# Where the squares of a head norm are split: at the end of each third, with root and product per half

## The chip, the cores and the metric

The kernel runs on one core of one Trainium2 chip. The metric is the device time of one execution in microseconds (us). Before the change it is 837.59 us, the median of three runs (837.31 to 838.25).

A core has five engines with a queue of instructions each, which they work through in order: TensorE (matrix products; its weight loads are shown apart as PEld), VectorE (DVE), ScalarE (ACT), GpSimd (POOL) and SyncE, which here only issues DMAs. Matrix products write to PSUM; this kernel uses four single PSUM banks (`bk0` to `bk3`) in turn, and two double ones for attention scores (`sc`).

## The reference

Two transformer-like layers work on 512 latent tokens and 256 context tokens of width 1024. The change lies in the first layer's mixer, differential attention with eight heads:

```python
def diff(qq, kk, vv, gate):
    o1 = sweep_attention(qq[..., 0, :], kk[..., 0, :], vv)
    o2 = sweep_attention(qq[..., 1, :], kk[..., 1, :], vv)
    o = o1 - lam.astype(o1.dtype) * o2
    o = rms_norm(o, subln_g) * (1.0 - lam_init)
    o = o.reshape(o.shape[0], o.shape[1], BRANCH_WIDTH)
    return (o * jax.nn.silu(gate)) @ w_out
```

The norm is `x * rsqrt(mean(x * x) + 1e-6) * g`, over the 128 channels of one head, for each of the 768 tokens. The second layer is grouped-query attention with norms on q and k; all is in float32.

## The kernel before, in words

Numbers are kept in float32, but TensorE multiplies them as pairs of a reduced type (`F32R`): a high part (a copy to that type, on ACT) and a low part (the difference between the number and its high part, on POOL or DVE). A product of two split numbers is three matmuls (`mm3`, L146 to L148); a product with ones needs two, one for each part.

In the first layer channels lie on the 128 partitions and tokens on the free axis. For each of the eight heads there are projections for q and k (`qk_proj`), v for two heads at a time (`v_proj`) and the gate z with its SiLU (`z_proj`), all of them called filling work here. Attention runs in three thirds of 256 tokens (`ch` 0 to 2): `s_units` makes scores and both softmaxes (DVE takes the maximum at L873, ACT the exponential at L876, POOL scales the first map at L214, DVE combines the two at L884), and `pv_steps` transposes the probabilities into a bank (L933), splits them (`ah` on ACT at L936, `al` on DVE at L937) and multiplies them with v (L153). The last matmul of a third leaves 128 channels by 256 tokens in a bank `o`. Then ACT writes its squares into the head's tile `sq` (L954), DVE writes it, times the norm's gain, into `gT[h]` (L214), and the bank is free.

After the third third comes the head norm, `subln`, in two halves of 384 tokens. For each half `colsum` makes the high part of the squares (ACT, L372) and the low part (POOL, L373) and sums them over the partitions by two matmuls with a matrix of ones (L374, L375) into a bank `o2`; ACT takes the logarithm of the mean (L965) back into `sq`. Then one exponential of minus half of it on all 768 tokens (L967, ACT) gives the reciprocal root, and one product on DVE (L968) applies it to `gT[h]`. `gate_mul` multiplies with the SiLU of the gate (L827, POOL). For the last head `subln_last` does the same in two parts of 512 and 256 tokens, each with its own exponential and product (L980 to L986), and also splits the result for the output projection.

The order is set in two stages. `flow` merges five streams of steps (scores S, transposes T, products with v M, norms X, gate vectors A) with the filling work, by due times and lags written as constants; a norm is due 2.5 (in the planner's own time) after the last product of its head. Then the framework's scheduler lays out each engine's queue by a rank: program order, moved ahead by the offset of the stream, which is 4200 for S, 3100 for T, 0 for M and 4800 for X (`HOT0`); the evacuation of q and k has 5400 (`WARM`). Filling work has none.

Small tiles come from a pool of three buffers with the tag "tmp": the rotary swap `sw`, the scratch `za` of the SiLU, and the parts `sqs` of the squares. `sq` has one buffer, which a head uses from its first third to the end of its norm. The four banks are handed out in turn, the one longest free first.

Of the kernel before, what the change touches and what calls it, by code (L numbers as in the profile page):

```python
# [9 lines left out]
F32 = mybir.dt.float32  # L10
F32R = mybir.dt.float32r
AF = mybir.ActivationFunctionType
ALU = mybir.AluOpType
# [3 lines left out]
P = 128  # L17
# [4 lines left out]
T = 768  # L22
# [57 lines left out]
def f32(ap):  # L80
    return ap.bitcast(F32)
# [3 lines left out]
def tile_backbone(  # L85
# [20 lines left out]
    nc = tc.nc  # L106
    uid = [0]

    def nm(s):
        uid[0] += 1  # L110
        return f"{s}_{uid[0]}"
# [15 lines left out]
    def trp():  # L127
        i = lru.pop(0)
        lru.append(i)
        return banks[i]  # L130

    def pj(n):
        i = lru.pop(0)
        o = banks[i][:, :n]
        held[id(o)] = (o, i)
        return o

    def close(o):
        lru.append(held.pop(id(o))[1])
# [10 lines left out]
    def pv_mm(o, vh, vl, c, ah, al, kt, first, last):  # L150
        terms = [(v, a, e) for v, a in ((vh, ah), (vl, ah), (vh, al)) for e in range(2)]
        for i, (v, a, e) in enumerate(terms):
            nc.tensor.matmul(o, v[:, kt + e, c], a[:, e * 256:e * 256 + 256], start=first and i == 0, stop=last and i == 5)  # L153
# [5 lines left out]
    ones_r = con.tile([P, P], F32R, name="ones_r")  # L159
    nc.vector.tensor_copy(ones_r, ones)  # L160
    eps = con.tile([P, 1], F32, name="eps")
# [48 lines left out]
    def scaled(eng, dst, src, s_):  # L210
        if eng == "a":
            nc.scalar.activation(dst, src, AF.Copy, scale=s_)
        else:
            (nc.vector if eng == "v" else nc.gpsimd).tensor_scalar(dst, src, s_, 1.0, ALU.mult, ALU.mult)  # L214
# [141 lines left out]
    def chunk(layer, tstep, mstep, kts, after, ts, ms):  # L356
        for i, kt in enumerate(kts):
            t = Step(lambda kt=kt: tstep(kt), 0.44, [(s_, LA[layer]) for s_ in after])
            if i:
                t.lag.append((ts[-1], LT[layer]))  # L360
            if len(ms) >= AB:
                t.lag.append((ms[-AB], 0.0))
            m = Step(lambda kt=kt: mstep(kt), 0.65, [(t, LM[layer])])
            ts.append(t)
            ms.append(m)
# [4 lines left out]
    def colsum(o, src, parts):  # L370
        hi, lo = parts
        nc.scalar.copy(hi, src)  # L372
        nc.gpsimd.tensor_tensor(lo, src, f32(hi), ALU.subtract)  # L373
        nc.tensor.matmul(o, ones_r, hi, start=True, stop=False)  # L374
        nc.tensor.matmul(o, ones_r, lo, start=False, stop=True)  # L375
# [11 lines left out]
    def rstd_sum(ssq, rest):  # L387
        r = small()
        nc.gpsimd.tensor_tensor(r, ssq, rest, ALU.add)  # L389
        nc.gpsimd.tensor_tensor(r, r, mhalf[:, :1], ALU.pow)  # L390
        return r
# [37 lines left out]
    def htile():  # L429
        return hp.tile([P, T], F32R, tag="h", name=nm("h"), bufs=16)  # L430
# [272 lines left out]
    gT = [None] * KT  # L703

    with tc.tile_pool(name="t0", bufs=1) as t0:
# [64 lines left out]
        def qr_tile():  # L770
            return t0.tile([P, T], F32, tag="qr", name=nm("qr"), bufs=4)
# [52 lines left out]
        def gate_mul(h):  # L824
            done.add(h)
            if h in szt and (h, "o") in done:
                nc.gpsimd.tensor_tensor(gT[h], gT[h], szt[h], ALU.mult)  # L827
# [96 lines left out]
        def pv_steps(h, at, ch, after, ts, ms):  # L924
            kts = range(6) if ch < 2 else range(4, 6)
            st = {}

            def tstep(kt):
                tr = trp()
                for e in range(2):  # L930
                    j = kt + e - kts[0]
                    for i, a in enumerate(at):
                        nc.tensor.transpose(tr[:, e * 256 + i * P:e * 256 + (i + 1) * P], a[:, j * P:(j + 1) * P], ident)  # L933
                ah = t0.tile([P, 512], F32R, tag="ah", name=nm("ah"), bufs=AB)
                al = t0.tile([P, 512], F32R, tag="al", name=nm("al"), bufs=AB)
                nc.scalar.copy(ah, tr)  # L936
                nc.vector.tensor_tensor(al, tr, f32(ah), ALU.subtract)  # L937
                st[kt] = ah, al

            def mstep(kt):  # L940
                if kt == kts[0]:
                    st["o"] = pj(256)
                o = st["o"]
                ah, al = st[kt]
                vh, vl = vt[h]
                vc = slice((h % 2) * P, (h % 2) * P + P)
                pv_mm(o, vh, vl, vc, ah, al, kt, kt == kts[0], kt == kts[-2])
                if kt == kts[-2]:
                    if ch == 2:
                        pvdone.add(h)  # L950
                    sl = slice(ch * 256, ch * 256 + 256)
                    if ch == 0:
                        ogs[h] = t0.tile([P, T], F32, tag="sq", name=nm("sq"), bufs=1)
                    nc.scalar.activation(ogs[h][:, sl], o, AF.Square)  # L954
                    scaled(EG0, gT[h][:, sl], o, subg)
                    close(o)

            chunk(0, tstep, mstep, kts[::2], [after], ts, ms)

        def subln(h):  # L960
            sq, og = ogs[h], gT[h]
            for (a, b) in halves:
                o2 = pj(384)
                colsum(o2, sq[:, a:b], [t0.tile([P, 512], F32R, tag="tmp", name=nm("sqs"), bufs=3)[:, :b - a] for _ in range(2)])
                nc.scalar.activation(sq[:, a:b], o2, AF.Ln, scale=1.0 / P, bias=eps)  # L965
                close(o2)
            nc.scalar.activation(sq, sq, AF.Exp, scale=-0.5)  # L967
            nc.vector.tensor_tensor(og, og, sq, ALU.mult)  # L968
            done.add((h, "o"))
            gate_mul(h)  # L970

        def subln_last(a, b):
            h = KT - 1
            sq, og = ogs[h][:, a:b], gT[h][:, a:b]
            if a == 0:
                ghi.append(htile())
                glo.append(htile())
            o2 = pj(b - a)
            colsum(o2, sq, [t0.tile([P, 512], F32R, tag="tmp", name=nm("sqs"), bufs=3)[:, :b - a] for _ in range(2)])
            nc.scalar.activation(sq, o2, AF.Ln, scale=1.0 / P, bias=eps)  # L980
            close(o2)
            nc.scalar.activation(sq, sq, AF.Exp, scale=-0.5)
            nc.vector.tensor_tensor(og, og, sq, ALU.mult)
            VP[EGL].tensor_tensor(og, og, szt[h][:, a:b], ALU.mult)
            nc.scalar.copy(ghi[h][:, a:b], og)
            nc.vector.tensor_tensor(glo[h][:, a:b], og, f32(ghi[h][:, a:b]), ALU.subtract)  # L986
# [29 lines left out]
        ogs = {}  # L1016
# [3 lines left out]
        for which, o in enumerate((oq, ok)):  # L1020
            r = qr_tile()
# [63 lines left out]
        for h in range(KT):  # L1085
# [33 lines left out]
            if h < KT - 1:  # L1119
                subs[h] = Step(lambda h=h: subln(h), 1.3, [(M_[-1], 2.5)])  # L1120
                X_.append(subs[h])
            else:
                for a, b, i in ((0, 512, -2), (512, 768, -1)):
                    X_.append(Step(lambda a=a, b=b: subln_last(a, b), 0.9, [(M_[i], 2.5)], ready=lambda: clock[0] if len(ghi) >= KT - 1 else None))
# [38 lines left out]
    for qi, (c, n) in enumerate(OUTC[:2]):  # L1163
# [4 lines left out]
        for m in order:  # L1168
            v = 0 if m < NQ else 1
            o = pj(n) if qi else o_pre[m]  # L1170
# [12 lines left out]
    c, n = OUTC[2]  # L1183
# [47 lines left out]
    for i, m in enumerate(order):  # L1231
        o = pj(n)
# [11 lines left out]
    with tc.tile_pool(name="t1", bufs=1, side="right") as t1p:  # L1244
# [61 lines left out]
        for what, m in KV:  # L1306
# [5 lines left out]
            else:  # L1312
                if what == "v" and wv is None:
                    wv = (ws.get(10), ws.get(11))
                o = pj(256)
# [227 lines left out]
        for qi, (c, n) in enumerate(OUTC1):  # L1543
# [4 lines left out]
            for m in range(NQ):  # L1548
                o = pj(n) if qi else o_pre[m]
# [12 lines left out]
                if qi == 2:  # L1562
                    r = rstd_sum(ss[m][:, 2:3], ss[m][:, 0:1])
                    for j in (1, 0):
                        for h in range(2 if m == NQ - 1 else 1):
                            w_ = 256 if m == NQ - 1 else 512
                            a = h * w_
                            sl = slice(j * 512 + a, j * 512 + a + w_)
# [90 lines left out]
```

## Time and profile before

| quantity | value |
|---|---|
| median of three runs | 837.59 us |
| the profiled execution, own time | 836.02 us |
| its span, first to last instruction | 834.0 us |
| granted TensorE clock, mean | 0.992 |
| TensorE busy | 797.1 us, 5482 matmuls |
| DVE, ACT, POOL busy | 484.2, 458.7, 437.0 us |

A row of a view names the line of the kernel, the engine, the operation and the tiles as out<-in; then comes, by view, a count, the busy time, the mean or a duration. "Idle before" and "waits" say how long an engine stood still and which instruction ended that. L12 is line 12 of the kernel before. The layer's eight heads run from about 105 to 480 us of the span.

### The profile page before, as it was taken

The page shows a single profiled execution, that of the slowest core. Times are in us where ns is not written, and L with a number is a line of the kernel's source. Part 1 is how long each engine was busy: PE and PEld are TensorE (multiplying, and loading weights), DVE is VectorE, ACT ScalarE, POOL GpSimd, SP SyncE. Part 2 cuts the span into 40 slices and gives each one's busy share as a digit, 9 for nine tenths or more (in the row PEclk, how much of TensorE's full clock was granted, in tenths as well). Part 3 has the DMA queues.
Part 4 walks back from the last instruction along what each step waited for, and adds up shares of the span by engine and source line. Part 5 has one row for each costly group of instructions (what it writes and reads, how often), then busy time and mean ns, then how long its engine had stood idle before and what let it go on. Part 6 is the DMA issues. An engine that isn't in the chain of part 4 may idle for free. (4 is left out here: it accounts for less than half of the span.)

```text
span 834.0 us, 14405 instructions
## 1 busy us (share of the span) xinstructions
PE 797.1 (96%) x5482; PEld 705.2 (85%) x5482; DVE 484.2 (58%) x897; ACT 458.7 (55%) x1001; POOL 437.0 (52%) x538
## 2 busy tenths in 40 slices
PE   7999999999999999999999999989998989999997
PEld 5788887798878898778988898779998779889986
DVE  4434576764857425665377843674266677665634
ACT  5424357674574644764467643754364656666731
POOL 4444755865475743765633212585776836723201
PEclk9899999999999999999999999999999999999999
DMA  9934211222133321414310051031232240300112
GB/s 302 353 112 140 76 39 47 63 95 70 71 102 127 114 76 64 151 42 153 124 51 26 27 202 51 26 108 51 77 99 79 81 153 21 102 26 26 64 38 101
DMA packets 41540, 77.77 MB, mean 93 GB/s; under 512 B 3584, under 2 KB 18688, under 8 KB 41472
## 3 DMA queue, kind: packets, MB, share of 16 engines
q1 hardware_dynamic: 38048, 71.71, 26.0%
q10 hardware_dynamic: 3424, 5.15, 1.8%
q8 instruction: 43, 0.70, 0.3%
q14 instruction: 25, 0.20, 0.1%
HBM read 70.56 MB, written 2.10 MB: 87 GB/s over the span
## 5 line engine op out<-in xcount | busy, mean ns | idle before, releaser
L200 POOL TENSOR_TENSOR wlo<-raw,whi 128x256 fp32r<-128x256 f32 x200 | 150.6, 784 | 89.1 <-ACT whi L206 75.6
L146 PE MATMUL bk<-whi,h 128*128 128x256 f32 (+1 forms) x592 | 177.0, 302 | 6.2 <-DVE u L1191 1.8
L147 PE MATMUL bk<-wlo,h 128*128 128x256 f32 (+1 forms) x592 | 176.3, 299 | 0.2 <-DVE wlo L200 0.2
L148 PE MATMUL bk<-whi,h 128*128 128x256 f32 (+1 forms) x592 | 175.0, 298 | 0.9 <-DVE h L1229 0.8
L146 PE MATMUL bk<-h,whi 128*128 128x512 f32 (+2 forms) x416 | 147.7, 355 | 2.4 <-ACT sq L965 1.5
L148 PE MATMUL bk<-h,wlo 128*128 128x512 f32 (+2 forms) x416 | 144.9, 349 | 0.1
L147 PE MATMUL bk<-h,whi 128*128 128x512 f32 (+2 forms) x416 | 144.9, 349 | 0.0
L146 PEld LDWEIGHTS bk<-whi,h 128*128 128x128 f32 x592 | 112.6, 190 | 16.4 <-issue 4.2
L147 PEld LDWEIGHTS bk<-wlo,h 128*128 128x128 f32 x592 | 112.6, 190 | 4.3 <-issue 0.5
L148 PEld LDWEIGHTS bk<-whi,h 128*128 128x128 f32 x592 | 111.9, 190 | 5.1 <-DVE h L1229 1.5
L214 POOL TENSOR_SCALAR p<-p,sm 128x768 f32<-128x768 f32 (+1 forms) x80 | 68.2, 855 | 82.0 <-DVE sm L879 34.6
L146 PEld LDWEIGHTS bk<-h,whi 128*128 128x128 f32 x416 | 78.2, 188 | 15.3 <-issue 4.5
L206 ACT CAST whi<-raw 128x1024 fp32r<-128x1024 f32 x64 | 67.4, 1053 | 37.2 <-DMA raw<-in_b_w 15.1
L148 PEld LDWEIGHTS bk<-h,wlo 128*128 128x128 f32 x416 | 78.1, 188 | 8.7 <-issue 1.3
L147 PEld LDWEIGHTS bk<-h,whi 128*128 128x128 f32 x416 | 78.3, 188 | 7.0 <-issue 0.8
L876 ACT ACTIVATE p<-sc,sm 128x768 f32<-128x768 f32 (+1 forms) x68 | 59.7, 882 | 29.4 <-DVE sm L873 28.7
L873 DVE TENSOR_REDUCE sm<-sc 128x1 f32<-128x768 f32 (+1 forms) x68 | 60.5, 919 | 22.2 <-PE sc L868 22.2
L184 POOL TENSOR_TENSOR sz<-sz,za 128x384 f32<-128x384 f32 (+1 forms) x24 | 28.1, 1173 | 39.3 <-ACT za L183 39.3
L936 ACT CAST ah<-bk 128x512 fp32r<-128x512 f32 x56 | 31.8, 592 | 29.5 <-PE bk L933 23.6
L937 DVE TENSOR_TENSOR al<-bk,ah 128x512 fp32r<-128x512 f32 x56 | 37.6, 684 | 16.0 <-ACT ah L936 15.5
L868 PE MATMUL sc<-qk,qk 64*128 64x384 f32 (+1 forms) x396 | 46.1, 355 | 0.2 <-POOL qk L768 0.2
L1430 DVE TENSOR_TENSOR al<-bk,ah 128x512 fp32r<-128x512 f32 x48 | 32.3, 685 | 23.0 <-ACT ah L1429 23.0
(245 smaller groups left out, 1700.1 us busy)
## 6 DMA issues: line engine op xcount, KB each, us to landing
raw<-in_a_w SPq DMA_DIRECT2D x30, 512.0 KB, 3.6
araw<-in_ada_w SPq DMA_DIRECT2D x12, 1024.0 KB, 5.5
raw<-in_b_w SPq DMA_DIRECT2D x20, 512.0 KB, 3.5
ag<-in_ada_w SPq DMA_DIRECT2D x32, 256.0 KB, 6.7
raw<-in_w_out SPq DMA_DIRECT2D x16, 512.0 KB, 3.5
sw<-qr ACTq DMA_DIRECT2D x32, 128.0 KB, 2.1
raw<-in_ada_w SPq DMA_DIRECT2D x8, 512.0 KB, 3.6
xt<-in_x SPq DMA_DIRECT2D x4, 512.0 KB, 5.3
```

Source lines behind the costliest of these rows:

```text
L146: nc.tensor.matmul(o, ahi, bhi, start=start, stop=False)
L147: nc.tensor.matmul(o, ahi, blo, start=False, stop=False)
L148: nc.tensor.matmul(o, alo, bhi, start=False, stop=stop)
L200: eng.tensor_tensor(dst[:, i:i + n], a[:, i:i + n], b[:, i:i + n], op)
L206: nc.scalar.copy(hi, r)
L214: (nc.vector if eng == "v" else nc.gpsimd).tensor_scalar(dst, src, s_, 1.0, ALU.mult, ALU.mult)
L868: prev = nc.tensor.matmul(sc[m][:, j if nk == T else m, :w], a[r, tok], b[r, c], start=i == 0, stop=i == 2)
L873: nc.vector.tensor_reduce(mx, scv, AX.XY if nk == T else AX.X, ALU.max, negate=True)
L876: nc.scalar.activation(pv_, scv, AF.Exp, bias=mx, accum_out=l[:, m:m + 1])
L936: nc.scalar.copy(ah, tr)
L937: nc.vector.tensor_tensor(al, tr, f32(ah), ALU.subtract)
L1430: nc.vector.tensor_tensor(al, tr, f32(ah), ALU.subtract)
```

## The change

At the end of each third the squares now go to a short-lived "tmp" buffer of 256 columns, and are split there and then: ACT copies the high part into the head's tile `sqh`, POOL subtracts for the low part `sql`. These instructions belong to the third's step. The norm's step keeps the two matmuls with ones per half, the logarithm, the exponential and the product; exponential and product are made per half, on a "tmp" buffer, and no longer on the tile of squares. `subln_last` uses the same helper for its two parts. `sqh` and `sql` have one buffer each, in place of the one of `sq`.

```diff
                     if ch == 0:
-                        ogs[h] = t0.tile([P, T], F32, tag="sq", name=nm("sq"), bufs=1)
-                    nc.scalar.activation(ogs[h][:, sl], o, AF.Square)
+                        ogs[h] = [t0.tile([P, T], F32R, tag=t, name=nm(t), bufs=1) for t in ("sqh", "sql")]
+                    sqh, sql = (t[:, sl] for t in ogs[h])
+                    sq = t0.tile([P, 512], F32, tag="tmp", name=nm("sq"), bufs=3)[:, :256]
+                    nc.scalar.activation(sq, o, AF.Square)
                     scaled(EG0, gT[h][:, sl], o, subg)
                     close(o)
+                    nc.scalar.copy(sqh, sq)
+                    nc.gpsimd.tensor_tensor(sql, sq, f32(sqh), ALU.subtract)
...
+        def sub_rstd(og, sqh, sql):
+            n = og.shape[-1]
+            o2 = pj(n)
+            nc.tensor.matmul(o2, ones_r, sqh, start=True, stop=False)
+            nc.tensor.matmul(o2, ones_r, sql, start=False, stop=True)
+            r = t0.tile([P, 512], F32, tag="tmp", name=nm("sr"), bufs=3)[:, :n]
+            nc.scalar.activation(r, o2, AF.Ln, scale=1.0 / P, bias=eps)
+            close(o2)
+            nc.scalar.activation(r, r, AF.Exp, scale=-0.5)
+            nc.vector.tensor_tensor(og, og, r, ALU.mult)
+
         def subln(h):
-            sq, og = ogs[h], gT[h]
+            og = gT[h]
             for (a, b) in halves:
-                o2 = pj(384)
-                colsum(o2, sq[:, a:b], [t0.tile([P, 512], F32R, tag="tmp", name=nm("sqs"), bufs=3)[:, :b - a] for _ in range(2)])
-                nc.scalar.activation(sq[:, a:b], o2, AF.Ln, scale=1.0 / P, bias=eps)
-                close(o2)
-            nc.scalar.activation(sq, sq, AF.Exp, scale=-0.5)
-            nc.vector.tensor_tensor(og, og, sq, ALU.mult)
+                sub_rstd(og[:, a:b], *(t[:, a:b] for t in ogs[h]))
             done.add((h, "o"))
             gate_mul(h)
...
-            o2 = pj(b - a)
-            colsum(o2, sq, [t0.tile([P, 512], F32R, tag="tmp", name=nm("sqs"), bufs=3)[:, :b - a] for _ in range(2)])
-            nc.scalar.activation(sq, o2, AF.Ln, scale=1.0 / P, bias=eps)
-            close(o2)
-            nc.scalar.activation(sq, sq, AF.Exp, scale=-0.5)
-            nc.vector.tensor_tensor(og, og, sq, ALU.mult)
+            sub_rstd(og, *(t[:, a:b] for t in ogs[h]))
```

More of the change, by code (lines that the diff above doesn't have):

```diff
@@ L973, in subln_last @@
             h = KT - 1
-            sq, og = ogs[h][:, a:b], gT[h][:, a:b]
+            og = gT[h][:, a:b]
             if a == 0:
```

## The prediction

> **What bounds the kernel now.** I read the page first, then the busy times by stage, then the waits of TensorE (PE) in the first layer's head loop, then the lines of the head norm, and last the order of time around the two places where PE waits for that norm.
>
> ```profile
> span 834.0 us, 14405 instructions
> PE 797.1 (96%) x5482; PEld 705.2 (85%) x5482; DVE 484.2 (58%) x897; ACT 458.7 (55%) x1001; POOL 437.0 (52%) x538
> ```
>
> ```profile
> 105.00:475.00 370.00, 360.58 (x2544) 312.71 (x2543) 234.20 (x407) 223.47 (x470) 210.70 (x210) 1.00 0.24 81
> ```
>
> The second row has busy PE, PEld, DVE, ACT, POOL, then the granted clock. The eight heads lie in this stretch. PE is busy for 360.58 of 370 us at a granted clock of 1.00, while ACT has 146.5 us free, POOL 159.3 and DVE 135.8. So work on ACT, POOL and DVE costs time only through a wait of PE. Those waits, from 105 to 490 us:
>
> ```profile
> PE bk L933 <- DVE al L937: 1.9, 2, 1.6
> PE bk L375 <- POOL sqs L373: 1.6, 1, 1.6
> PE bk L146 <- ACT sq L965: 1.5, 1, 1.5
> PE bk L724 <- DVE al L937: 0.9, 1, 0.9
> ...
> PE sc L868 <- POOL qk L768: 0.2, 1, 0.2
> ```
>
> Columns: total, times, longest. The whole answer has twelve rows and 9.3 us (1.9, 1.6, 1.5, 0.9, 0.7, 0.6, 0.5, 0.5, 0.4, 0.3, 0.2, 0.2). Two of them, 3.1 us, are waits for the head norm: one for the low part of the squares (L373 on POOL), one for the root (L965 on ACT). That is about all that a quicker norm can give back directly: 0.4% of the time.
>
> **The change, part by part.** The instructions concerned, with minimum, median and maximum ns:
>
> ```profile
> L954 ACT ACTIVATE sq<-bk x24: 376/386/405, 115.2 to 480.4; 128x256 f32<-128x256 f32 x24
> L372 ACT CAST sqs<-sq x16: 408/514/619, 129.4 to 480.9; 128x384 fp32r<-128x384 f32 x14, 128x512 fp32r<-128x512 f32 x1, 128x256 fp32r<-128x256 f32 x1
> L373 POOL TENSOR_TENSOR sqs<-sq,sqs x16: 736/1012/1609, 131.6 to 481.4; 128x384 fp32r<-128x384 f32 x14, 128x512 fp32r<-128x512 f32 x1, 128x256 fp32r<-128x256 f32 x1
> L967 ACT ACTIVATE sq<-sq x7: 842/848/867, 138.6 to 453.8; 128x768 f32<-128x768 f32 x7
> L968 DVE TENSOR_TENSOR gT<-gT,sq x7: 951/1272/2050, 139.4 to 454.7; 128x768 f32<-128x768 f32 x7
> L983 DVE TENSOR_TENSOR gT<-gT,sq x2: 426/560/694, 478.3 to 485.9; 128x512 f32<-128x512 f32 x1, 128x256 f32<-128x256 f32 x1
> ```
>
> ```profile
> L180 ACT ACTIVATE za<-za 128x384 f32<-128x384 f32 (+1 forms) x24 | 13.6, 566 | 0.4
> ```
>
> *High and low parts.* Per head, two copies of 384 columns (0.514) and two subtractions (1.012) become three of 256, whose durations are the minima of L372 and L373: 0.408 and 0.736. ACT: 3 x 0.408 - 2 x 0.514 = +0.20 us per head. POOL: 3 x 0.736 - 2 x 1.012 = +0.18. The last head has three copies in place of a 512 and a 256: the same +0.2. Over eight heads: ACT +1.6, POOL +1.5.
>
> *Root and product per half.* One Exp of 768 (0.848) becomes two of 384, priced by L180, an Exp of 384: 2 x 0.566 - 0.848 = +0.28 us of ACT in seven heads, +2.0. One product of 768 (0.951 undisturbed, 1.272 median) becomes two, each at the mean of the 512 and 256 products (0.560): 1.12, so between -0.15 and +0.17 per head on DVE. Ln stays two of 384.
>
> *Load.* ACT +3.6 us in the loop against 146.5 free, POOL +1.5 against 159.3, DVE about 0. PE has the same products with ones. No DMA is added, removed or moved past another. If the cover of ACT goes at a place, the transposes' copies (L936, "ah") are late next, and behind them the PSUM bank that PE waits for in L933 and L724: three waits above. One added copy of 0.408 in front of each makes +1.2 at the worst, 0 at the best. Most ACT gaps are elsewhere, so I take +0.4.
>
> *The first wait of PE, head 0.* In order of time:
>
> ```profile
> 128.88 2.81 POOL L200 TENSOR_TENSOR wlo<-raw,whi 128x256 fp32r<-128x256 f32 x4 [1.21 <-ACT whi L206]
> 129.39 0.52 ACT L372 CAST sqs<-sq 128x384 fp32r<-128x384 f32 x1
> ...
> 130.75 0.33 PE L374 MATMUL bk<-sqs,ones_r 128*128 128x384 f32 x1
> 130.95 0.39 ACT L954 ACTIVATE sq<-bk 128x256 f32<-128x256 f32 x1 [1.05 <-PE bk L153]
> ...
> 131.64 2.12 POOL L373 TENSOR_TENSOR sqs<-sq,sqs 128x384 fp32r<-128x384 f32 x2
> ...
> 132.71 0.44 PE L375 MATMUL bk<-sqs,ones_r 128*128 128x384 f32 x1 [1.62 <-POOL sqs L373]
> 132.81 0.19 PEld L146 LDWEIGHTS bk<-h,whi 128*128 128x128 f32 x1
> ```
>
> PE starts the pair with the high part at 130.75 and then stands 1.62 us, because POOL is still on four pieces of a weight split. The first half of the head needs the first third (Square at 115.2) and half of the second. After the change the first third's low part is long there, but the second third's still follows the weight split: 131.64 + 0.74 = 132.38 against 132.65. If the pair keeps its place in PE's order, only 0.27 us is won; if PE's order sets it behind the z matmuls that now follow, all 1.62. No row tells which; I take the middle, -0.9.
>
> *The second wait, head 6.*
>
> ```profile
> 442.94 0.39 ACT L954 ACTIVATE sq<-bk 128x256 f32<-128x256 f32 x1
> ...
> 451.48 1.07 ACT L936 CAST ah<-bk 128x512 fp32r<-128x512 f32 x2 [2.40 <-PE bk L933]
> 452.44 0.60 ACT L965 ACTIVATE sq<-bk,eps 128x384 f32<-128x384 f32 x1
> ```
>
> ```profile
> 444.29 1.01 POOL L373 TENSOR_TENSOR sqs<-sq,sqs 128x384 fp32r<-128x384 f32 x1 [4.44 <-ACT sqs L372]
> 447.39 1.02 POOL L184 TENSOR_TENSOR sz<-sz,za 128x384 f32<-128x384 f32 x1 [2.10 <-ACT za L183]
> 448.39 0.91 POOL L214 TENSOR_SCALAR p<-p,sm 128x768 f32<-128x768 f32 x1
> 449.27 1.00 POOL L373 TENSOR_TENSOR sqs<-sq,sqs 128x384 fp32r<-128x384 f32 x1
> ```
>
> ```profile
> 448.82 0.34 PE L374 MATMUL bk<-sqs,ones_r 128*128 128x384 f32 x1
> ...
> 453.09 0.45 PE L146 MATMUL bk<-h,whi 128*128 128x384 f32 x1 [1.47 <-ACT sq L965]
> ```
>
> The last third's Square ends at 443.33, yet the second half's low part is made at 449.27, behind two other POOL jobs, and the root then queues behind two "ah" copies; the sum's bank is held from 448.82 to 453.04 and the next projection needs it. With the parts made at the third's end, copy and subtraction (0.41 + 0.74) fit into POOL's idle time before 447.39, and pair and root follow some 5 us earlier. I take the whole 1.47 away; the other end is 0, should another bank be late in its place.
>
> *The squares' buffer.* Square now writes a "tmp" buffer (three, shared with the rotary swap and the SiLU scratch) instead of one buffer per head. New wait: Square behind the last reader of that buffer, and behind Square on ACT everything queued, with PE waiting for the bank that Square reads. I take 0, since it needs three holders at once, and price it as a rival.
>
> *A rule against it.* DVE's combining of the two probability tiles took longer while POOL subtracted:
>
> ```profile
> 435.06 1.00 DVE L884 SCALAR_TENSOR_TENSOR p<-p,sm,p 128x768 f32<-128x768 f32 x1
> ...
> 449.34 1.75 DVE L884 SCALAR_TENSOR_TENSOR p<-p,sm,p 128x768 f32<-128x768 f32 x1 [0.75 <-POOL p L214]
> ```
>
> The Trainium skill ("GPSIMD Engine Reference", section "Specifications") says that POOL shares its SBUF interfaces with VectorE and collides with DVE instructions that read two SBUF inputs. The trace agrees, 1.75 against 1.00 us with the subtraction at 449.27 beside it. By that rule POOL's added 1.5 us would put at most 1.5 us on DVE; were all of it on PE's path, the sum would be 837.1 instead of 835.6.
>
> *Sum.* -0.9 - 1.47 + 0.4 = -2.0 us. The profiled execution took 836.02 us (its span 834.0 and 2.0 around it), 1.57 below the median 837.59; I carry the difference over to the median: 837.59 - 2.0 = 835.6. Best ends: -1.62 - 1.47 and the two LDWEIGHTS waits for L372 (1.8 us, mostly beside matmuls):
>
> ```profile
> PEld sc L868 <- ACT sqs L372: 1.0, 3, 0.4
> ...
> PEld bk L146 <- ACT sqs L372: 0.8, 1, 0.8
> ```
>
> that is -4.9, or 832.7. My case itself runs from 832.7 to 835.9.
>
> **Rivals.** *A, slower: the pair waits for POOL at more heads.* Copy and subtraction leave the norm's step (order offset 4800, ahead of softmax at 4200) for the third's step (offset 0), while the products with ones keep 4800. On POOL the subtraction can then stand behind whatever is ahead: a four-piece split is 2.81 us, a probability scaling 0.91. Head 0 shows what PE pays when it reaches the pair first: 1.62. With k such heads the time is 837.59 - 1.47 + 0.4 + 1.62 x (k - 1): 838.1 for two, 839.8 for three, 841.4 for four. It decides from three heads on. For it: the one stall of this kind is there with the subtraction at the highest rank. Against it: a third's subtraction is 0.27 us shorter, and two of the three are early.
>
> *B, no change: waits move.* Only 3.1 of 9.3 us belong to the norm, and PE's fixed order is laid anew around every pair; a bank freed here is waited for elsewhere (the "al" waits, 2.8 us). 837.6, between 835.9 and 839.3. For it: PE is at 97% of the stretch.
>
> *C, slower: Square waits for "tmp".* In the last head two SiLU scratch tiles are held when a Square comes, here ACT's rows and then POOL's:
>
> ```profile
> 459.09 0.53 ACT L179 ACTIVATE za<-sz 128x384 f32<-128x384 f32 x1
> ...
> 466.93 0.57 ACT L179 ACTIVATE za<-sz 128x384 f32<-128x384 f32 x1
> ...
> 471.21 0.39 ACT L954 ACTIVATE sq<-bk 128x256 f32<-128x256 f32 x1 [0.73 <-PE bk L153]
> ```
>
> ```profile
> 468.55 1.45 POOL L184 TENSOR_TENSOR sz<-sz,za 128x384 f32<-128x384 f32 x1 [4.14 <-ACT za L183]
> ...
> 473.95 1.20 POOL L184 TENSOR_TENSOR sz<-sz,za 128x384 f32<-128x384 f32 x1
> ```
>
> The second is free only at 475.15, so one buffer of three is left for Square and the root together. A user more makes Square wait for such a POOL job, 1.2 us each; with three such waits on PE's path and nothing won, 837.6 + 3.6 = 841.2. Against it: it needs a third holder, and the first scratch is free at 470.00, ahead of that Square.
>
> **How the numbers follow.** Forecast 0.42, A 0.34, B 0.20, C 0.04. 0.2% is 1.7 us, about what a measurement of this kernel can tell from no change; the cases were cut there, so faster 0.42, same 0.20, slower 0.38. The time is that of the likeliest case, 835.6. The range, 832.7 to 841.4, takes in the best ends and A with four heads; more heads and C with more waits lie outside.
>
> **What would show it.** Right: no PE wait for the root of head 6, the pairs with ones next to each other, the bank held for a pair and its root (about 0.34 + 0.34 + 0.60) and no longer 4.2 us as in head 6, ACT busy 3.6 us more. Wrong: PE waits in the low product, each behind a POOL row, at three heads or more (A); the wait sum near 9 us with other names (B); Square idle behind POOL or DVE (C). The forecast also fails if a wait that has nothing to do with the norm, at the layer's end or in the second layer, grows because the order was laid anew.

## The result, and the profile after

| | before | after |
|---|---|---|
| median, measured side by side | 837.75 us | 845.69 us |
| lowest and highest of six | 837.31 to 838.41 | 843.94 to 848.11 |
| profiled execution, own time | 836.02 us | 843.94 us |

The ratio after to before is 1.0098, with a 95% interval from 1.0085 to 1.0112. The change makes the kernel slower by 7.9 us. The forecast was 835.6 us, with a range to 841.4.

The totals of the page of the changed kernel, with the same matmuls as before:

```profile
span 842.1 us, 14445 instructions
PE 800.1 (95%) x5482; PEld 705.8 (84%) x5482; DVE 489.2 (58%) x904; ACT 458.2 (54%) x1016; POOL 443.8 (53%) x546
```

No engine became the bound. ACT shows 458.2 us against 458.7, DVE 5 us more, POOL 6.8 us more. The span is 8.1 us longer. PE's busy time, for the same matmuls, accounts for 3.0 of them, and its idle time for 5.1. So the loss lies in waits of PE and, for a part, in matmuls that took longer. In the changed kernel the Square is L956, the copy L959, the subtraction L960, the products with ones L967 and L968, the logarithm L970, the exponential L972, the product L973; other lines of the head loop up to there have kept their numbers. The waits of PE from 105 to 490 us (total, times, longest):

```profile
PE bk L933 <- DVE al L937: 2.8, 4, 0.9
PE bk L933 <- DVE p L884: 2.2, 2, 1.8
PE bk L933 <- DVE mods L423: 1.9, 1, 1.9
PE sc L868 <- ACT p L907: 1.4, 1, 1.4
PE sc L897 <- ACT p L876: 1.1, 1, 1.1
...
```

There are thirteen rows and 13.6 us, against twelve and 9.3 before. Both waits for the norm, 3.1 us, are gone, as forecast; no row has L968 or L970. What came in their place waits for the softmax (`p`), for the split probabilities (`al`) and once for a modulation vector (`mods`). No row that is new names the norm.

Where in the layer it happens can be read from the Square, which marks the end of each third in both kernels. Its rows for the changed kernel, and the twelfth of the 24 Squares in each, before first:

```profile
L956 ACT ACTIVATE sq<-bk x24: 374/386/417, 115.6 to 489.5; 128x256 f32<-128x256 f32 x24
```

```profile
274.68 0.39 ACT L954 ACTIVATE sq<-bk 128x256 f32<-128x256 f32 x1 [0.24 <-PE bk L153]
```

```profile
278.13 0.39 ACT L956 ACTIVATE sq<-bk 128x256 f32<-128x256 f32 x1 [0.27 <-PE bk L153]
```

The first Square is 0.4 us late (115.2 before, 115.6 after), the twelfth 3.45, the last 9.1 (480.4 and 489.5). So some 3 us are lost early and some 6 later, all inside the eight heads. The early loss, in order of time: ACT, POOL and PE of the changed kernel, while the first head ends and the second is prepared.

```profile
115.61 0.38 ACT L956 ACTIVATE sq<-bk 128x256 f32<-128x256 f32 x1
115.77 1.12 ACTq L759 DMA_DIRECT2D sw<-qr  x2
116.94 0.90 ACT L876 ACTIVATE p<-sc,sm 128x768 f32<-128x768 f32 x1 [0.94 <-POOL p L214]
117.98 0.98 PE L897 MATMUL sc<-qk,qk 64*128 64x256 f32 x12 [1.08 <-ACT p L876]
118.49 1.78 POOL L760 TENSOR_TENSOR qr<-qr,rope 128x512 f32<-128x512 f32 x1 [1.66 <-DMA sw<-qr]
120.23 0.73 POOL L960 TENSOR_TENSOR sql<-sq,sqh 128x256 fp32r<-128x256 f32 x1
122.88 3.58 POOL L768 TENSOR_TENSOR qk<-qr,qk 128x768 fp32r<-128x768 f32 x2
124.40 0.45 PE L868 MATMUL sc<-qk,qk 64*128 64x384 f32 x2 [1.36 <-ACT p L907]
```

The same instructions before:

```profile
107.68 0.47 ACTq L759 DMA_DIRECT2D sw<-qr  x1
...
108.18 0.62 ACTq L759 DMA_DIRECT2D sw<-qr  x1
...
115.18 0.39 ACT L954 ACTIVATE sq<-bk 128x256 f32<-128x256 f32 x1
...
116.50 0.98 PE L897 MATMUL sc<-qk,qk 64*128 64x256 f32 x12
```

```profile
110.40 1.83 POOL L760 TENSOR_TENSOR qr<-qr,rope 128x512 f32<-128x512 f32 x1 [1.40 <-DMA sw<-qr]
118.33 3.64 POOL L768 TENSOR_TENSOR qk<-qr,qk 128x768 fp32r<-128x768 f32 x2 [1.87 <-ACT qk L767]
```

The rotary swap of the next head (two DMAs, issued by ACT at L759) went out at 107.68, while ACT had time. Now it goes out at 115.77, right behind the Square. Two things follow. The second of the two Exps (L876) starts only at 116.94, when both DMAs have been issued (115.77 + 1.12 = 116.89), and PE waits 1.08 us for it. The row names POOL's scaling as what ended ACT's idle time; I read it as the issues. In the kernel before this Exp began at 115.46, ahead of the scaling (115.56), so it does not need it. And in two of the experiments below, which show the same sequence, the Exp again starts 0.05 us after the issues end, while the distance from the end of the scaling varies (0.10 and 0.03). And the chain behind the swap on POOL (L760, then the split of q and k, L768) is late: L768 begins at 122.88 and not at 118.33. Of these 4.55 us, 0.73 are the new subtraction L960 that stands in between.

PE's 1.36 us at L868 ended with the exponentials L907 on ACT and not with L768. They were late through DVE, which has work of the swap in its queue as well:

```profile
119.03 1.26 DVE L883 TENSOR_TENSOR sm<-sm,nlam 128x1 f32<-128x1 f32 x1
...
121.71 1.28 DVE L903 TENSOR_REDUCE sm<-sc 128x2 f32<-128x512 f32 x2
```

L903 is the maximum that L907 waits for; before, it began at 117.88. Now the swap's product on DVE (L761, 0.69 us) stands ahead of it. So does the one-column L883, which took 0.16 us before, and now ends 0.02 us after POOL's L760 (118.49 + 1.78 = 120.27).

The later loss: DVE's combining of the probabilities and POOL's split of q and k, before,

```profile
351.98 1.02 DVE L884 SCALAR_TENSOR_TENSOR p<-p,sm,p 128x768 f32<-128x768 f32 x1 [0.22 <-POOL p L214]
...
352.51 4.33 POOL L768 TENSOR_TENSOR qk<-qr,qk 128x768 fp32r<-128x768 f32 x2 [0.56 <-ACT qk L767]
```

and after, with PE:

```profile
357.27 4.32 POOL L768 TENSOR_TENSOR qk<-qr,qk 128x768 fp32r<-128x768 f32 x2
357.34 2.57 DVE L884 SCALAR_TENSOR_TENSOR p<-p,sm,p 128x768 f32<-128x768 f32 x1 [1.00 <-POOL p L214]
359.96 0.56 PE L933 MATMUL bk<-ident,p 128*128 128x128 f32 x3 [1.83 <-DVE p L884]
```

L884 used to begin 0.53 us ahead of L768. Now it begins 0.07 us behind it, takes 2.57 us in place of 1.02, and PE stands 1.83 us. The stop is followed by a second cost, in the windows of one us each (busy PE, PEld, DVE, ACT, POOL, then the granted clock):

```profile
358.00:359.00 1.00, 0.13 (x1) 0.00 (x0) 1.00 (x1) 0.00 (x0) 1.00 (x1) 1.00 0.92 369
...
360.00:361.00 1.00, 1.00 (x6) 1.00 (x7) 1.00 (x2) 0.46 (x2) 1.00 (x1) 0.68 0.00 0
361.00:362.00 1.00, 1.00 (x5) 1.00 (x4) 0.27 (x2) 1.00 (x7) 0.72 (x2) 0.50 0.00 0
362.00:363.00 1.00, 1.00 (x5) 1.00 (x4) 0.33 (x2) 1.00 (x6) 0.79 (x2) 0.50 0.08 16
363.00:364.00 1.00, 1.00 (x6) 1.00 (x5) 0.84 (x2) 1.00 (x4) 0.00 (x0) 0.61 0.00 0
```

PE runs at about half clock for some 3.4 us after it stood. That is 0.32 + 0.50 + 0.50 + 0.39 = 1.7 us more. A second stop comes soon after:

```profile
371.14 0.66 PE L933 MATMUL bk<-ident,p 128*128 128x128 f32 x4 [1.89 <-DVE mods L423]
```

The wait ends with the second of two small operations of DVE (L423, at 370.94), which in its queue is behind a product of the SiLU (L182) and a softmax maximum (L873). From 345 to 375 us PE now loses 1.83 + 1.7 + 1.89 = 5.4 us, and lost 1.5 before: some 4 of the 6 us.

### The profile page after: what moved, and what is told of

Same layout as the page of the kernel before. It is cut to its first block, busy times and chain, and to the rows that moved or that the text cites. A ratio compares the mean times of both kernels' runs of the same rounds, so it can differ in the third digit from the quotient of the medians.

```text
span 842.1 us, 14445 instructions
## 1 busy us (share of the span) xinstructions
PE 800.1 (95%) x5482; PEld 705.8 (84%) x5482; DVE 489.2 (58%) x904; ACT 458.2 (54%) x1016; POOL 443.8 (53%) x546
## 5 line engine op out<-in xcount | busy, mean ns | idle before, releaser
L200 POOL TENSOR_TENSOR wlo<-raw,whi 128x256 fp32r<-128x256 f32 x200 | 152.6, 795 | 82.7 <-ACT whi L206 69.0
L876 ACT ACTIVATE p<-sc,sm 128x768 f32<-128x768 f32 (+1 forms) x68 | 59.7, 879 | 48.0 <-DVE sm L873 46.4
L873 DVE TENSOR_REDUCE sm<-sc 128x1 f32<-128x768 f32 (+1 forms) x68 | 60.8, 918 | 24.0 <-PE sc L868 23.9
L868 PE MATMUL sc<-qk,qk 64*128 64x384 f32 (+1 forms) x396 | 45.8, 354 | 2.3 <-ACT p L907 1.4
L884 DVE SCALAR_TENSOR_TENSOR p<-p,sm,p 128x768 f32<-128x768 f32 (+1 forms) x34 | 42.3, 1243 | 8.1 <-POOL p L214 5.7
```

The costliest lines, as they stand in the source:

```text
L200: eng.tensor_tensor(dst[:, i:i + n], a[:, i:i + n], b[:, i:i + n], op)
L868: prev = nc.tensor.matmul(sc[m][:, j if nk == T else m, :w], a[r, tok], b[r, c], start=i == 0, stop=i == 2)
L873: nc.vector.tensor_reduce(mx, scv, AX.XY if nk == T else AX.X, ALU.max, negate=True)
L876: nc.scalar.activation(pv_, scv, AF.Exp, bias=mx, accum_out=l[:, m:m + 1])
L884: nc.vector.scalar_tensor_tensor(ps_[0], pt, r, ps_[0], ALU.mult, ALU.add)
```

## The experiments

**The theory to be tested.** The tag "tmp" has three buffers, which are handed out in program order. Square's tile is asked for at the third's end, which in the program stands ahead of the next head's rotary swap, though the swap has the higher rank (offset 5400 against 0). Since the swap's tile comes out of the same tag behind the Square's, the swap can no longer be moved ahead of the Square. The rivals are those of the prediction: A, the low part itself is late on POOL and PE pays for it; C, three buffers are too few.

**First set: which tile of the tag does it.** One kernel has both new tiles on tags of their own, two have only one of them there, and one keeps both in "tmp" with four buffers:

```diff
-                    sq = t0.tile([P, 512], F32, tag="tmp", name=nm("sq"), bufs=3)[:, :256]
+                    sq = t0.tile([P, 256], F32, tag="sqt", name=nm("sq"), bufs=2)
...
-            r = t0.tile([P, 512], F32, tag="tmp", name=nm("sr"), bufs=3)[:, :n]
+            r = t0.tile([P, 512], F32, tag="sr", name=nm("sr"), bufs=1)[:, :n]
```

Both on their own:

> The changed kernel, but the squares' short-lived tile has two buffers of its own and the root's tile one of its own, so that neither takes a tmp buffer. Theory (the buffers of a tag are handed out in program order, so the rotary swap of the next head, which is ranked first, must wait for the Square, which is ranked last): the swap is issued ahead of the first third's Square again, the loss of 7.9 us goes, 835 to 839 us. Rival A (parts at the third's end, low rank on POOL, are the cause): nothing of the loss goes, 844 to 847. Rival N (every new order costs by chance): anywhere from 838 to 848, with other waits.

Square alone on its own:

> The changed kernel, with buffers of its own for the squares' tile alone; the root's tile stays in tmp. Theory: most of the loss goes, since it is the Square that the swap waits for at heads 0 and 4; the swap behind the two roots (heads 4 and 5) stays late: 836 to 841 us. Rival A: 844 to 847. Rival N: 838 to 848.

The root's tile alone on its own:

> The changed kernel, with a buffer of its own for the root's tile alone; the squares' tile stays in tmp. Theory: the swap of head 0 stays behind the Square, so at least the 3 us lost there stay: 841 to 846 us. Rival A: 844 to 847, as in the changed kernel. Rival N: 838 to 848.

Four buffers (`bufs=4` at every tile of "tmp"):

> The changed kernel, with four tmp buffers in place of three. Theory (order of handing out, no shortage): no gain, 844 to 847 us. Rival C (three buffers are too few, Square and swap wait for a buffer to come free): the loss goes for the most part, 836 to 841.

Measured, with the first swap and the first Square of the head loop in each trace:

| kernel | median us | ratio, 95% interval | swap issued | Square |
|---|---|---|---|---|
| before (837.1 in this set) | | | 107.68 | 115.18 |
| after | 845.69 | 1.0098 (1.0085 to 1.0112) | 115.77 | 115.61 |
| both on their own | 838.49 | 1.0018 (1.0008 to 1.0028) | 108.41 | 115.93 |
| Square's tile on its own | 839.5 | 1.0023 (1.0011 to 1.0035) | 109.58 | 117.09 |
| root's tile on its own | 844.0 | 1.0083 (1.0066 to 1.0101) | 115.89 | 115.73 |
| four buffers | 847.06 | 1.0120 (1.0097 to 1.0142) | 116.62 | 116.49 |

Square's tile carries nearly all of it. In the kernels of this set that keep it in "tmp" the swap comes behind the Square, and the time is 844 us or more; a fourth buffer brings nothing back (847.06 us, just past the 847 that the theory gave). So it is not a shortage (C): the order is fixed before any buffer is full. Nor does the swap wait for the Square's own buffer: in the changed kernel it goes out 0.16 us after the Square begins, and the last reader of that buffer (L960) ends at 120.96. A falls too, since the low part is made at the same step in all four kernels.

**Second set: the parts one by one, and the cause without the change.** The kernel before with the root and the product per half:

```diff
                 nc.scalar.activation(sq[:, a:b], o2, AF.Ln, scale=1.0 / P, bias=eps)
                 close(o2)
-            nc.scalar.activation(sq, sq, AF.Exp, scale=-0.5)
-            nc.vector.tensor_tensor(og, og, sq, ALU.mult)
+                nc.scalar.activation(sq[:, a:b], sq[:, a:b], AF.Exp, scale=-0.5)
+                nc.vector.tensor_tensor(og[:, a:b], og[:, a:b], sq[:, a:b], ALU.mult)
```

> The kernel before with one part of the change alone: the power of -1/2 and the product with the head are made per half; Square, the parts and their buffers stay as before. Theory (what was lost was the order in which buffers of tag tmp are handed out, and this run hands out none in another order): between 835.5 and 838.5 us, with the wait of TensorE near 453 us shortened or gone if the forecast's second gain of 1.5 us was real, and there if it was not. Rival (the two halves' roots and products themselves cost time on ScalarE and VectorE): 839 to 842 us.

Measured 836.73 us beside 837.3, ratio 0.9995 (0.9979 to 1.0011): no difference. The wait for the root of head 6 is where it was, so this part does not give it back:

```profile
455.96 0.44 PE L146 MATMUL bk<-h,whi 128*128 128x384 f32 x1 [1.47 <-ACT sq L965]
```

The kernel before with the parts at the third's end, in buffers that are not of "tmp", root and product on the whole head:

```diff
-                        ogs[h] = t0.tile([P, T], F32, tag="sq", name=nm("sq"), bufs=1)
-                    nc.scalar.activation(ogs[h][:, sl], o, AF.Square)
+                        ogs[h] = [t0.tile([P, T], F32, tag="sq", name=nm("sq"), bufs=1)] + [t0.tile([P, T], F32R, tag=t, name=nm(t), bufs=1) for t in ("sqh", "sql")]
+                    sq, sqh, sql = (t[:, sl] for t in ogs[h])
+                    nc.scalar.activation(sq, o, AF.Square)
                     scaled(EG0, gT[h][:, sl], o, subg)
                     close(o)
+                    nc.scalar.copy(sqh, sq)
+                    nc.gpsimd.tensor_tensor(sql, sq, f32(sqh), ALU.subtract)
...
```

> The kernel before with the other part alone: Square writes the head's own buffer as before, the high and low parts are made at the end of each third into buffers of their own, and the root and product stay on the whole head; no tile of tag tmp is used by the norm any more. Theory: the parts cost what is left over in the run with both tiles on their own tags, so 837 to 840 us, with the wait of TensorE near 133 us still there because the low part of the last third is made as late as before. Rival (the parts at the third's end cost the 8 us): 843 to 846 us. Forecast's own claim (the wait at 133 us goes): 835.5 to 837 us.

Measured 836.57 us, ratio 0.9987 (0.9977 to 0.9997). The parts at the third's end don't cost the 8 us. The time is below the 837 to 840 us of the theory, and in the range that went with the forecast's own claim, but the claim itself fails. Near 133 us, POOL and PE of this kernel:

```profile
133.08 1.42 POOL L959 TENSOR_TENSOR sql<-sq,sqh 128x256 fp32r<-128x256 f32 x2
...
133.85 0.45 PE L968 MATMUL bk<-sql,ones_r 128*128 128x384 f32 x1 [1.64 <-POOL sql L959]
```

PE still stands 1.64 us for the low part (1.62 before): the second third's subtraction follows the weight split, as before. The wait for the root of head 6 is gone here, but PE waits 0.9 us for the gain product and 0.8 for a weight's low part in its place, from 425 to 490 us:

```profile
...
PE bk L146 <- DVE gT L214: 0.9, 1, 0.9
PE bk L147 <- DVE wlo L200: 0.8, 1, 0.8
```

The kernel before with nothing but a user of "tmp" at the third's end, one column that nothing reads:

```diff
                     nc.scalar.activation(ogs[h][:, sl], o, AF.Square)
+                    cold = t0.tile([P, 512], F32, tag="tmp", name=nm("cold"), bufs=3)[:, :1]
+                    nc.scalar.copy(cold, ogs[h][:, ch * 256:ch * 256 + 1])
                     scaled(EG0, gT[h][:, sl], o, subg)
```

> The kernel before with the suspected cause alone: after each third's Square one column is copied into a new tile of tag tmp that nothing reads, so that a buffer of that tag is asked for at the third's end; no part of the change is in it, the sum is unchanged. The added work is 24 copies of one column on ScalarE, some 0.2 to 0.3 us each. Theory: the rotary swaps of the next heads are issued late as in the changed kernel, 842 to 847 us. Rival (the parts on ScalarE and GpSimd or the roots per half cost the time, not the order of the buffers): 837 to 840 us.

Measured 849.57 us, ratio 1.0143 (1.0125 to 1.0161), slower than the change itself and past the upper end of what the theory gave. And its control in the third set, the same 24 copies into a tag of their own (`tag="cold"`, 8 columns):

> The control to the run with the unread column in tag tmp (849.6 us): the same 24 copies of one column at the same places, but into a tag of their own, so that they take no buffer of tag tmp. The sum is unchanged. Theory (the order in which tmp buffers are handed out costs the time, not the copies): 837 to 840 us. Rival (24 small copies on ScalarE at the third's end cost it): 845 to 850 us.

Measured 835.71 us beside 836.65, ratio 0.9983 (0.9973 to 0.9993), a little below what was expected. The two kernels differ by the tag of an unread tile (and the width of its buffer, 512 and 8 columns), and by some 13 us: one is 12.3 us above the kernel before of its set, the other 0.9 below. ACT's rows, first with the tile in "tmp" and then with it apart:

```profile
115.77 0.39 ACT L954 ACTIVATE sq<-bk 128x256 f32<-128x256 f32 x1
...
116.71 0.47 ACTq L759 DMA_DIRECT2D sw<-qr  x1
...
117.29 0.21 ACT L956 COPY cold<-sq 128x1 f32<-128x1 f32 x1
```

```profile
110.22 0.47 ACTq L759 DMA_DIRECT2D sw<-qr  x1
...
117.73 0.39 ACT L954 ACTIVATE sq<-bk 128x256 f32<-128x256 f32 x1
...
119.25 0.21 ACT L956 COPY cold<-sq 128x1 f32<-128x1 f32 x1
```

This is the plainest of the runs: no part of the change is in it, and the swap is late all the same.

The changed kernel with the swap, not the Square, taken out of the tag:

```diff
-                sw = t0.tile([P, 512], F32, tag="tmp", name=nm("sw"), bufs=3)
+                sw = t0.tile([P, 512], F32, tag="sw", name=nm("sw"), bufs=2)
```

> The changed kernel with one tile moved: the rotary swap's tile gets a tag of its own with two buffers, Square and root stay in tag tmp. Theory (the swap was late because its buffer came after the Square's): the swap is issued at 107 to 109 us again and the time is 837 to 841 us. Rival (what is late is the Square, the root or the low part itself, and the swap only shows it): 843 to 847 us.

Measured 837.17 us beside 837.3, ratio 0.9994 (0.9985 to 1.0003); the swap is issued at 109.05, the Square comes at 116.56. So one buffer tag brings back all of the loss, and leaves no gain.

**Third set: is there a gain left?** The whole change with Square and root in the head's own buffer, so that the norm has no tile of "tmp" (the two edits of the second set together):

> The whole change without a tile of tag tmp: parts at the end of each third, root and product per half, but Square and root use one buffer per head as before. Theory: both parts alone gave 836.6 and 836.7 us, so together 835.5 to 838 us. Rival (parts and roots per half disturb each other, as the 838.5 us of the run with both tiles on tags of two and one buffers may say): 838 to 840 us.

Measured 837.39 us beside 836.65, ratio 1.0006 (0.9994 to 1.0017). The kernel before with the swap on its own tag:

> The kernel before with only the rotary swap on a tag of its own with two buffers. It asks whether the swap waits for tag tmp in the kernel before already, behind the parts of the squares. Theory (there the parts have a rank near the swap's own, and the swap came ahead of them at heads 0 and 4): 836 to 838 us, no difference to measure. Rival (tag tmp holds it up before as well): 832 to 835.5 us.

Measured 836.85 us, ratio 1.0001 (0.9988 to 1.0014): the tag does not hold up the swap in the kernel before. The parts alone, with the subtraction on VectorE (`nc.vector` for `nc.gpsimd`):

> The kernel with the parts alone in buffers of their own (836.6 us), with the subtraction on VectorE in place of GpSimd. It asks whether the wait of TensorE near 133 us, which stayed in every run with the swap in its place, goes when the low part is not behind GpSimd's four-piece weight split. Theory: that wait goes, 24 subtractions are added to VectorE's free time, 834.5 to 836.5 us. Rival (VectorE's softmax is pushed back and TensorE waits for it instead): 837 to 841 us.

Measured 841.65 us, ratio 1.0061 (1.0044 to 1.0078). Near the first pair, PE:

```profile
130.94 0.33 PE L967 MATMUL bk<-sqh,ones_r 128*128 128x384 f32 x1
...
131.14 0.45 PE L968 MATMUL bk<-sql,ones_r 128*128 128x384 f32 x1
```

The wait that all runs with an early swap kept is gone: the low product follows the high one at once. But PE's waits from 105 to 490 us are now led by DVE's other work:

```profile
PE bk L933 <- DVE al L937: 2.7, 3, 1.6
PE bk L153 <- DVE al L937: 2.2, 4, 0.7
```

The rival of that run holds, a little past its upper end of 841 us: it moves the wait and costs 5 us.

No version is clearly better than the kernel before. The two lowest, the parts alone (0.9987) and the control with 24 useless copies (0.9983), stand equally far below it; as useless copies do as well, a newly laid order can be worth 1 us here by itself. It is not worth 8, though, which answers rival N of the first set. Apart from the kernel with the subtraction on VectorE, the eight with an early swap lie between 835.71 and 839.5 us, and the four with a late one between 844.0 and 849.57.

## Why the prediction was wrong

**The step that failed** is the squares' buffer: "I take 0, since it needs three holders at once". The resource was the right one and the mechanism the wrong one. I asked when the buffer would be full, and there the answer of 0 is right: four buffers gave no gain (847.06 us). What counts is the order of the hand-out. A tile asked for at rank 0 stands between tiles of ranks 4800 and 5400 of the same tag, and the higher one has to follow it. Its price is some 8 us in the change (845.69 us beside 837.75; with the swap moved out 837.17 beside 837.3), and some 13 us for the bare hand-out. Of the DMAs the prediction asked only whether one is "moved past another"; the swap's first one was issued 8.1 us later (107.68 and 115.77).

**The load** was rightly taken as hidden. Its sizes were off on POOL. Its groups, changed kernel first, then before:

```profile
L960 POOL TENSOR_TENSOR sql<-sq,sqh 128x256 fp32r<-128x256 f32 x23 | 22.2, 969 | 30.9 <-ACT sqh L959 24.6 <-DVE mods L424 6.3
```

```profile
L373 POOL TENSOR_TENSOR sqs<-sq,sqs 128x384 fp32r<-128x384 f32 x14 | 14.8, 1054 | 15.6 <-ACT sqs L372 14.1 <-issue 1.1
```

A subtraction of 256 columns takes some 0.74 us undisturbed, as priced, but 1.3 to 1.5 where it begins behind an L884 of DVE that is still at work, and so 0.97 in the mean. POOL's total grew by 6.8 us and not 1.5. On ACT I forecast 3.6 us more and the page shows 0.5 less; on DVE about 0, and it shows 5.0 more.

**The first wait** (-0.9) was a choice between 0.27 and 1.62. With the swap early, all five kernels with the parts at the third's end on POOL still stand there, for 1.33 to 1.64 us. The lower end was right, or nothing: PE comes to the pair at the same place, and the second third's low part is still behind the weight split. In the changed kernel the wait is gone because everything is laid otherwise: PE takes the low products only at 138.69, behind other matmuls, the prediction's second case.

**The second wait** (-1.47) was right as a mechanism: gone in the change, in the parts alone and with either tag mended, and there with the root per half alone. It did not become time: in the parts alone 0.9 + 0.8 us of other waits came up, and with both tiles on their own tags PE waits 0.7 us for the root of another head. That is rival B, and the change without a tile of "tmp" ended where B put it, at no difference (837.39 us; B said 837.6).

**The rivals.** The result lies on the slower side, to which I gave 0.38, but not by A: no PE wait for a low product is in the changed kernel, let alone three. C named the tag, at 0.04, and gave its price (841.2) by another mechanism. What the prediction left unasked is which higher ranked step shares a tag with the step that was given a lower rank; its own text names the sharers, "the rotary swap and the SiLU scratch".

**The rule of the Trainium skill** ("GPSIMD Engine Reference", "Specifications") was priced as at most 1.5 us through the added subtractions. On this trace it acted elsewhere: L884 took 2.57 us beside L768, and the stop of PE behind it was 1.83 us. L768 is not an added instruction; it was moved. What counts in these traces is which of the two begins first. Before and after, 13 of the L884 on 768 columns overlap a POOL subtraction, sum or product that began later, and take 1.01 or 1.02 us, as alone. The 19 that begin behind one take 1.37 to 2.59 us and end some 0.8 us after it.

What stays open: why the bare hand-out costs 4 us more than the change (849.57 and 845.69). A part of it may be the clock. In the profiled executions, from 105 to 511 us, the clock is at a half for 13.7 us with the bare hand-out and for 3.4 in the change, which costs 6.8 and 1.7 us. But that execution, of 852.24 us, is the slowest of its four. In the bare hand-out the parts `sqs` are still users of the tag besides the new one, so that the norm takes seven tiles of it in a head, and five in the change; that this is the reason was not tried. Nor is it shown, link by link, how the late swaps lead to the order near 357 us; only that the stop behind L884 there is absent when Square and root, or the swap, leave the tag. It is absent too with the root's tile alone on its own tag, which still takes 844.0 us, with a stop of 1.7 us for split probabilities (`al`) instead. So that one stop does not carry the loss.

## What to carry to other kernels

Before a tile is put into a shared tag, list who else takes buffers of that tag and at which rank: a low ranked user that stands earlier in the program can hold back the higher ranked ones behind it, here with three buffers and with four. Not every such user costs time: the SiLU scratch has no rank and shares the tag in the kernel before, and with the swap apart that kernel is no faster (836.85 us). To test it, add a one-column tile that nothing reads, once in the tag and once beside it. And price a stop of PE, where it is long, at more than its own length.

## What was not expected

After a stop of PE of about 1.6 us or more the granted clock can fall to a half for some 3.4 us. The changed kernel showed it at 360 us, above. The same stop does not always do it: after its stop of 1.89 us at 371 us the clock stays at 1.00. Nor does it after the wait for the low part of head 0 in the kernel before, but it does in the one with both tiles on their own tags:

```profile
132.00:133.00 1.00, 0.29 (x2) 0.30 (x3) 0.42 (x2) 1.00 (x4) 0.90 (x2) 1.00 0.31 49
...
134.00:137.00 3.00, 3.00 (x19) 2.84 (x17) 1.49 (x2) 1.99 (x4) 0.83 (x2) 1.00 0.15 60
```

```profile
133.00:134.00 1.00, 0.00 (x0) 0.00 (x0) 1.00 (x3) 1.00 (x3) 1.00 (x2) 1.00 0.00 0
134.00:135.00 1.00, 0.64 (x2) 0.64 (x3) 0.05 (x1) 1.00 (x4) 1.00 (x3) 0.74 0.57 57
135.00:138.00 3.00, 3.00 (x11) 3.00 (x11) 2.27 (x4) 1.10 (x3) 0.88 (x1) 0.52 0.43 161
```

After 1.62 us the first stays at 1.00; after 1.64 us the second falls to 0.52 and loses 0.26 + 3 x 0.48 = 1.7 us. So a stop of 1.6 us costs 1.6 us in the one execution and 3.3 in the other. It fits with this that one and the same kernel spreads: with the root per half, twelve executions lie between 833.92 us at a mean clock of 0.995 and 840.69 at 0.988. The slow stretch can also be twice as long: with the unread column in "tmp" it lasts from 124.7 to 131.6 us.

The Trainium skill ("TensorE: Matmul & The Clock Gate", "What's actually happening") tells of a free-running window of about 3.4 us, at whose end an idle array goes to half clock. The length of the slow stretch and its chance nature agree. The Trainium skill asks there for a whole idle window before the clock falls; here a stop of half a window was enough (1.64 us).
